# Layer B's first products of a hybrid trunk: right operands split one and a half products ahead, S2 staggered, row stores moved by two products, the fourth operand's split moved one product

## The chip, the cores and the metric

The kernel runs on one core of a Trainium2 chip. The metric is the device time of one execution in microseconds (us), the median of three runs. The profile and the trace belong to one profiled execution, and its times are counted from the start of that execution's span.

## The reference, cut to what matters

Two layers are applied to a sequence of 1024 tokens of width 1024, each as `h = h + W_out(mixer(RMSNorm(h)) * silu(z))`; a final RMSNorm follows.

```python
hn = rmsnorm(h, norm_w[0])
z, u, v = split(hn @ a_w_in, 3)                  # 1024 x 6144, layer A
mixed = einsum(w_causal, layernorm(v)) + b_s     # chunks of 128 tokens
h = h + (u * mixed * silu(z)) @ a_w_out          # 2048 x 1024
hn = rmsnorm(h, norm_w[1])
proj = hn @ b_w_in                               # layer B: z (2048), x (2048), B and C (1024 each), dt (32)
xbc = silu(causal_depthwise_conv(x, B, C))       # 4 taps
# chunked state-space scan over 128-token chunks, gate by silu(z), grouped RMSNorm
h = h + gated @ b_w_out
out = rmsnorm(h, final_norm_w)
```

The change lies in the middle: the end of layer A's output product, and the part of `proj` that gives z and half of x, B and C.

## The kernel before, in words

**Products.** Large matrix products are done by one level of a seven-product scheme (Winograd's form of Strassen's): left and right operand are cut into 2 x 2 blocks, sums of blocks are formed, and seven half-size products, numbered 1 to 7, are added up into the four results C11, C12, C21, C22. The matmuls take their operands in the type fp32r. To keep the accuracy of float32, each operand is split into a high part (a cast on ACT, `hh` on the left and `wh` on the right, in `split`, L111, or L109 where the sign is turned) and a low part (the rest, a subtraction on DVE, `hl` and `wl`, L112 or L110). A product is then three matmuls, high by high, low by high and high by low (`mm3`, L134, L135, L136).

**Class `Block`.** One Block is one set of columns of a weight matrix. Its right operands come from four loaded quarters (`load`, queued by SP, L120). `prep(n)` makes product n's `wh` and `wl`; both come from pools with three buffers. `sums_a` and `sums_b` begin the operand sums t1 and t2: ACT writes a negated quarter (L211, L212, L217), then DMAs queued by POOL add other quarters to it in memory (L202). Product 6 uses t2, product 5 t1. `mm(n, i)` does one half (`unit`) of product n, 12 matmuls of 128 x 512; products 6 and 7 go on adding to the accumulators of product 1, so these must have been copied away first. `post(n, i)` does what follows a half: for products 1, 6 and 7 an ACT copy of the accumulator to `u` (L292), for the others a result: a DVE sum (L972 for z columns, L1320 for x, B and C) and what is to be done to it later.

**Results.** For z columns ACT applies Silu (L977) and stores on its own DMA queue (L978). For x, B and C the result goes through the four-tap convolution: one ACT pass (L1287), three DVE taps (L1281 with a few edge columns in L1284), then Silu (L1312) and a store (L1313), both on ACT.

**The stages around the change.** The order of each engine's instructions is the order in which the Python code issues them; in these stages it is written out by hand, and each engine is given its own list of it.

- Layer A's output product (class `Out`, 560 to 692 us) goes through products 1, 7, 2, 6, 4, 5, 3 in steps `c` of 0 to 3. At each step `hook_a` does side work; `store_h1(0, c, 0)` stores a row block of the new h on ACT's DMA queue (L913). At the end of product 6 ACT copies its four accumulators to `u` (L855), and product 4 adds to the same accumulators.
- `into_b` (692 to 775 us) normalises and transposes the rows of h, makes the left operands of layer B (A11, A12, A22, S1 to S4), and runs the seven products of the first z block in between. S2, the left operand of product 6, is made for four token tiles: a DVE difference (L1085), ACT's high part (L109) and DVE's low part (L110); the S3 differences are L1080.
- `blocks` (777 to 1040 us) runs six more blocks (z1, x01, z2, bc01, x35, bc35, each in the order 1, 2, 6, 7, 5, 4, 3) and the narrow block z3 (1, 2, 6, 5, 7, 3, 4). Between the halves come one step of the `decays` list (dt, softplus and cumulative sums, DVE L1215 to L1238) and the results that are waiting.
- After that come `scans` with the remaining projections (accumulators `ab`), to about 1440 us, and layer B's output product. The first of these projections needs the fourth left operand A21, which `rest_a21` reads back from DRAM (`f01`, `f` in the profile, SP L1337) and splits (ACT L111 and DVE L112 on 128 x 2048).

Of the kernel before, what the change touches and what calls it, by code (L numbers as in the profile page):

```python
# [29 lines left out]
def kernel(  # L30
# [34 lines left out]
    def s8(shape, name, dt=F32):  # L65
        return sb.tile(shape, dt, name=name, tag="s8", bufs=16)
# [39 lines left out]
    def split(hi, lo, src, eng=None, sign=1.0):  # L106

        if sign < 0:
            nc.scalar.mul(hi, src, sign)  # L109
            return nc.vector.scalar_tensor_tensor(lo, src, sign, hi.bitcast(F32), ALU.mult, ALU.subtract)  # L110
        nc.scalar.copy(out=hi, in_=src)  # L111
        return (eng or nc.vector).tensor_tensor(out=lo, in0=src, in1=hi.bitcast(F32), op=ALU.subtract)  # L112
# [491 lines left out]
    for g in range(G):  # L604
# [26 lines left out]
        def mix(m, th):  # L631
            c = g * 2 + m
            mx = sm("mx")
            for q in range(4):
# [11 lines left out]
        blk = Block(HS, lambda kh, j: [a_w_in[kh * 512:(kh + 1) * 512, j * DI + g * 256:j * DI + (g + 1) * 256]],  # L646
                    False, done_zu)
# [263 lines left out]
    def store_h1(th, tt, nb):  # L911
        queue = nc.sync if nb else nc.scalar
        queue.dma_start(out=h1_d[th * 4 + tt][:, nb * 512:(nb + 1) * 512], in_=ao.row(th, tt, nb))  # L913

    def hook_a(n, c):
        if n == 1:
            ao.fetch(1, min(c + 2, 3))
        elif n == 7:
            ao.fetch(2, c), ao.fetch(22, c)
        elif n in (2, 6, 4):  # L920
            if n > 2:
                ao.fetch({6: 4, 4: 5}[n], c)
                store_h1(0, c, 0) if n == 6 else None
            ao.sums(n, c)
            if (n, c) == (6, 3):
                ao.b12_plus(0, 0)
        else:
            ao.prep_last(c)
            store_h1(1, c, 0)

    def from_a():

        blk.prep(3)
        for c in range(2):
            ao.fetch(1, c)
        ao.prep(1, 0)
        mix(0, 1)
        blk.mm(3, 0)
        mix(1, 1)
        blk.mm(3, 1)  # L940
        for n in (1, 7, 2, 6, 4):
            for i, _ in enumerate(ao.product(n, hook_a)):
                if n == 1 and i in (0, 2):
                    mix(i // 2, 0)
                    if i == 2:
                        store()
# [12 lines left out]
    def finish():  # L959

        while late:
            late.pop(0)()
# [61 lines left out]
    def into_b():  # L1024
# [4 lines left out]
        blk = zb[0]  # L1029
        nrm, F, TP, st = {}, {}, {}, {}  # L1030
# [15 lines left out]
        def part(name, tt):  # L1046
            return [m[:, :, tt * P:(tt + 1) * P] for m in H2[name]]
# [29 lines left out]
        def s3(tt):  # L1077
            if tt == 0:
                st["s3"] = s8([P, 4, 4, P], "s3")
            TTv(out=st["s3"][:, tt], in0=F[1, tt][:, 0], in1=F[0, tt][:, 0], op=ALU.subtract)  # L1080

        def s2(tt):

            f0 = F[1, tt][:, 0]
            TTv(out=f0, in0=f0, in1=F[0, tt][:, 1], op=ALU.subtract)  # L1085
            split(*part("S2", tt), f0, sign=-1.0)
            if tt % 2:
                f = st[tt // 2]
                Gp.dma_start(out=f[:, :, 1], in_=f[:, :, 0], accum_op=ALU.add)
# [8 lines left out]
        for n, _ in enumerate(ao.product(5, hook_a)):  # L1098
            if n == 8:
                ao.prep_unit(0)  # L1100
# [50 lines left out]
        blk.fourth()  # L1151
        blk.eng = None
        blk.prep(4)
        s3(3)
        for i in range(2):
            blk.mm(2, i, False)
        for tt in range(4):
            s2(tt)
        blk.prep(6)
        blk.post(1, 0), blk.post(1, 1)  # L1160
        for tt in range(4):
            both("S3", tt, st["s3"][:, tt])
        dt_post(1, pd)
# [17 lines left out]
        nxt = zb[1]  # L1181
# [108 lines left out]
    def xbc_block(kind, gs):  # L1290

        held, halos = {}, {}

        def cols(j):
            if kind == "x":
                return [(DI + gs[j] * 256, 256)]
            return [(2 * DI + j * 1024 + g * P, P) for g in gs]

        def W(kh, j):
            return [b_w_in[kh * 512:(kh + 1) * 512, c:c + n] for c, n in cols(j)]  # L1300

        def out(th, i, j, src, halo=None):
            if kind == "x":
                g, m, c = gs[j], i, cols(j)[0][0] + i * P
            else:
                g, m, c = gs[i], 2 + j, cols(j)[i][0]
            dst = k2([P, 512], "xc")
            for op in conv_ops(dst, src, (c - DI) // P, halo):
                op()

            def rest():
                nc.scalar.activation(dst, dst, AF.Silu)  # L1312
                nc.scalar.dma_start(out=xbc_d[g][:, th, m, :], in_=dst)  # L1313

            return rest

        def done(name, i, a, u):
            th, j = 2 - int(name[1]), int(name[2]) - 1
            if u is not None:
                nc.vector.tensor_tensor(out=u, in0=a, in1=u, op=ALU.add)  # L1320
                a = u
            if th == 0:
                halo = halos[i, j] = tiny([P, 8], "halo")[:, 0:3]
                nc.vector.tensor_copy(out=halo, in_=a[:, 509:512])
                todo.append(lambda: out(0, i, j, a))
                if (i, j) in held:
                    todo.append(lambda: out(1, i, j, held[i, j], halo))
            elif (i, j) in halos:
                todo.append(lambda: out(1, i, j, a, halos[i, j]))
            else:  # L1330
                held[i, j] = a

        return Block(H2, W, False, done, None)

    def rest_a21():
        raw = s8([P, 4, 512], "f01")
        nc.sync.dma_start(out=raw, in_=f01_d)  # L1337
        yield
        H2.update(new_H(("A21",)))
        split(*H2["A21"], raw)  # L1340
# [79 lines left out]
    def blocks():  # L1420


        ORDER, LAST = (1, 2, 6, 7, 5, 4, 3), (1, 2, 6, 5, 7, 3, 4)
        for g in SPILT:
            xbc_d[g] = dr.tile([P, 2, 4, 512], F32, name=f"xbc_d{g}")
        pairs = SPILT[:2], SPILT[2:]
        bs = [zb[1], xbc_block("x", pairs[0]), zb[2], xbc_block("bc", pairs[0]), xbc_block("x", pairs[1]),
              xbc_block("bc", pairs[1]), zb[3]]
        seq = [(k, n) for k in range(len(bs)) for n in (ORDER if k < len(bs) - 1 else LAST)]
        small, turn, a21 = decays(), [0], rest_a21()  # L1430

        def unit(b, n, i):

            turn[0] += 1
            off = late[:]
            late.clear()
            if b is bs[-1]:
                if n in (1, 6, 7):
                    late.append(todo.pop(0)())
            elif next(small, 0) == 0 and todo and (turn[0] % 2 or len(todo) > 3):  # L1440
                late.append(todo.pop(0)())
            b.mm(n, i, b is not bs[-1] or n != 5)
            if b is bs[-1] and n == 7:
                b.post(5, i)
            for f in off:
                f()

        for at, (k, n) in enumerate(seq[1:], 1):
            b, nxt = bs[k], bs[k + 1] if k + 1 < len(bs) else None
            if at + 1 < len(seq):  # L1450
                k2_, n2 = seq[at + 1]
                if n2 not in bs[k2_].Y:
                    bs[k2_].prep(n2)
            if n == 2:
                b.fourth()
            if nxt is not None:
                if n == 1 or at == 1:
                    nxt.load(0, 1)
                if n == 6:
                    nxt.load(0, 0)  # L1460
                elif n == 7:
                    nxt.sums_a()
                elif n == 5:
                    nxt.load(1, 0)
                    nxt.sums_b()
                elif n == 4:
                    nxt.load(1, 1)
            elif n == 6:
                next(pj)
            elif n == 5:  # L1470
                next(a21)
            elif n == 4:
                next(pj)
            for i in range(b.units):
                unit(b, n, i)
        finish()
        next(a21, None)

    with tc.manual_schedule():
        into_b()  # L1480
        blocks()
# [482 lines left out]
```

## Time and profile before

| | |
|---|---|
| three runs | 1590.07, 1592.04, 1591.79 us; median 1591.79 |
| profiled execution | 1599.45 us, of which the span is 1597.6 us |
| TensorE (PE) busy | 1503.3 us, 94% of the span |
| DVE, ACT, POOL busy | 1063.6, 782.9 and 420.2 us |
| mean granted TensorE clock | 0.975 |
| output product of layer A | 560 to 692 us |
| `into_b` | 692 to 775 us |
| `blocks` | 777 to 1040 us |

The span is what the trace covers; the profiled execution's own time is 1.85 us longer, and 7.66 us (0.5%) above the median of the runs. PE stands for TensorE's matmuls, ACTq or SPq for the DMA issues of that engine, and `u<-acc` for an instruction that reads the tile `acc` and writes `u`. A bracket such as `[2.64 <-ACT u L292]` says that the engine sat idle for 2.64 us ahead of the instruction, and that the idle time was ended by ACT's instruction on line 292.

### The profile page before, as it was taken

What the parts mean: (1) busy time and instruction counts of PE and PEld (TensorE: products, weight loads), DVE (VectorE), ACT (ScalarE), POOL (GpSimd) and SP (SyncE); (2) the same over time, 40 slices, a digit from 0 to 9 for tenths busy, and PEclk for the clock granted to TensorE, in tenths of its full rate; (3) what the DMA queues carried; (4) which work ended last, traced back from release to release, by engine and by line L of the source; (5) the groups of instructions that cost most, each with busy time, mean ns of one, the idle gap of its engine ahead of it and who ended that gap; (6) DMA issues with size and microseconds to landing.
All of it is one profiled execution on the core that took longest, in us unless ns stands there. A gap on an engine that the chain in (4) does not pass through costs nothing.

```text
span 1597.6 us, 21214 instructions
## 1 busy us (share of the span) xinstructions
PE 1503.3 (94%) x7830; PEld 1239.6 (78%) x7830; DVE 1063.6 (67%) x1701; ACT 782.9 (49%) x1251; POOL 420.2 (26%) x441
## 2 busy tenths in 40 slices
PE   5799999999999999998999999989999999987997
PEld 4799988888888887776788787767777777766876
DVE  7976566666666644777737377646776666777876
ACT  4522232332323354655555555546666666755363
POOL 3601110000000131210011312116766666532121
PEclk8899999999999999999999999999999999998999
DMA  5154323322333999856367878666566464677872
GB/s 174 41 174 143 106 98 111 111 98 98 110 110 111 329 262 245 191 128 139 99 159 178 165 165 158 162 188 188 162 180 179 133 183 126 198 270 167 221 139 105
DMA packets 174839, 251.82 MB, mean 158 GB/s; under 512 B 16288, under 2 KB 102928, under 8 KB 171536
## 3 DMA queue, kind: packets, MB, share of 16 engines
q1 hardware_dynamic: 124120, 168.39, 33.9%
q0 software_dynamic: 39520, 63.19, 20.5%
q10 hardware_dynamic: 11096, 18.90, 3.3%
q8 instruction: 62, 1.02, 0.3%
q14 instruction: 41, 0.34, 0.1%
HBM read 185.61 MB, written 51.18 MB: 148 GB/s over the span
## 4 chain that ended last, share of the span: by engine, by line
PE 59%; issue 15%; DVE 10%; ACT 7%; DMA 6%; POOL 1%; SPq 1%; ACTq 1%; POOLq 0%; DVEq 0%
PE acc L136 10%; PE acc L134 9%; PE acc L135 9%; PE ab L134 4%; PE ab L136 4%; PE ab L135 4%; PE yy L1571 2%; PE yy L1575 2%; DVE wl L112 2%; PE bo L135 2%; PE bo L134 2%; PE bo L136 2%; PE ao L134 2%; PE ao L135 2%; PE ao L136 2%
## 5 line engine op out<-in xcount | busy, mean ns | idle before, releaser
L134 PE MATMUL acc<-hh,wh 128*128 128x512 f32 x868 | 343.2, 395 | 15.0 <-ACT u L292 7.2
L136 PE MATMUL acc<-hh,wl 128*128 128x512 f32 x868 | 341.7, 394 | 2.2 <-DVE wl L112 2.1
L135 PE MATMUL acc<-hl,wh 128*128 128x512 f32 x868 | 340.2, 392 | 0.0
L134 PEld LDWEIGHTS acc<-hh,wh 128*128 128x128 f32 x868 | 164.6, 190 | 51.9 <-ACT u L292 8.9
L112 DVE TENSOR_TENSOR wl<-wr,wh 128x1024 fp32r<-128x1024 f32 (+1 forms) x97 | 115.6, 1193 | 125.8 <-ACT wh L111 125.8
L136 PEld LDWEIGHTS acc<-hh,wl 128*128 128x128 f32 x868 | 164.5, 189 | 39.9 <-DVE wl L112 5.5
L135 PEld LDWEIGHTS acc<-hl,wh 128*128 128x128 f32 x868 | 164.5, 190 | 33.4
L111 ACT CAST wh<-wr 128x1024 fp32r<-128x1024 f32 (+1 forms) x113 | 116.5, 1031 | 103.1 <-PE acc L135 56.7
L292 ACT COPY u<-acc 128x512 f32<-128x512 f32 x117 | 67.7, 583 | 200.1 <-PE acc L136 198.5
L136 PE MATMUL acc<-wh,hl 128*128 128x256 f32 x448 | 131.7, 294 | 12.4 <-DVE hl L395 12.4
L134 PE MATMUL ab<-hh,wh 128*128 128x512 f32 x288 | 129.5, 450 | 7.2 <-DVE x L1281 3.8
L134 PE MATMUL acc<-wh,hh 128*128 128x256 f32 x448 | 132.5, 296 | 3.8 <-DVE vt L331 2.1
L135 PE MATMUL acc<-wl,hh 128*128 128x256 f32 x448 | 130.9, 292 | 1.3 <-DVE wl L405 1.3
L135 PE MATMUL ab<-hl,wh 128*128 128x512 f32 x288 | 114.3, 397 | 3.2 <-DVE hl L112 3.2
L136 PE MATMUL ab<-hh,wl 128*128 128x512 f32 x288 | 115.2, 400 | 0.0
L136 PEld LDWEIGHTS acc<-wh,hl 128*128 128x128 f32 x448 | 90.2, 201 | 13.5 <-DVE hl L395 13.5
L134 PEld LDWEIGHTS acc<-wh,hh 128*128 128x128 f32 x448 | 90.4, 202 | 4.8 <-ACT wh L111 2.3
L135 PEld LDWEIGHTS acc<-wl,hh 128*128 128x128 f32 x448 | 90.5, 202 | 1.7 <-DVE wl L405 1.5
L134 PE MATMUL bo<-wh,xh 128*128 128x512 f32 x192 | 78.5, 409 | 8.0 <-ACT wh L111 7.2
L112 DVE TENSOR_TENSOR xl<-ya,xh 128x1024 fp32r<-128x1024 f32 x40 | 49.9, 1246 | 53.1 <-ACT xh L111 53.1
L1544 ACT ACTIVATE wl<-wl,tk 128x128 f32<-128x128 f32 x256 | 81.5, 391 | 0.6 <-DMA wl<-cs_d 0.3
L645 POOL DMA_DIRECT2D y_d<-y x8 | 4.4, 548 | 290.9 <-DVE y L642 290.9
(320 smaller groups left out, 3284.0 us busy)
## 6 DMA issues: line engine op xcount, KB each, us to landing
wr<-in_a_w_in_dram SPq DMA_DIRECT2D x48, 512.0 KB, 3.8
wl<-cs_d SPq DMA_DIRECT2D x64, 256.0 KB, 3.4
wr<-in_b_w_in_dram SPq DMA_DIRECT2D x30, 512.0 KB, 5.1
wb<-in_a_w_out_dram SPq DMA_DIRECT2D x10, 1024.0 KB, 11.2
wb<-in_b_w_out_dram SPq DMA_DIRECT2D x10, 1024.0 KB, 8.0
wr<-in_b_w_in_dram SPq DMA_DIRECT2D x36, 256.0 KB, 5.7
v<-v_d SPq DMA_DIRECT2D x8, 1024.0 KB, 5.0
y_d<-y POOLq DMA_DIRECT2D x8, 1024.0 KB, 5.6
```

The lines of the kernel that those rows point to most:

```text
L111: nc.scalar.copy(out=hi, in_=src)
L112: return (eng or nc.vector).tensor_tensor(out=lo, in0=src, in1=hi.bitcast(F32), op=ALU.subtract)
L134: nc.tensor.matmul(out=o, lhsT=l[0], rhs=r[0], start=start, stop=False, **kw)
L135: nc.tensor.matmul(out=o, lhsT=l[0], rhs=r[1], start=False, stop=False, **kw)
L136: nc.tensor.matmul(out=o, lhsT=l[1], rhs=r[0], start=False, stop=stop, **kw)
L292: nc.scalar.copy(out=self.u[n][:, i], in_=a)
L645: store = lambda: nc.gpsimd.dma_start(out=y_d[-1], in_=y)
L1544: nc.scalar.activation(wl[:, j, :], wl[:, j, :], AF.Relu, scale=-1.0, bias=tokc(2, c, self.g)[:, j:j + 1])
L1571: nc.tensor.matmul(out=yy[f * 64:(f + 1) * 64, pt * P:(pt + 1) * P], lhsT=w[:, j * 64:(j + 1) * 64], rhs=wl[:, j, :], start=True, stop=True)
L1575: nc.tensor.matmul(out=yy[:, 256 + pt * P:384 + pt * P], lhsT=self.state[c - 1][:, pt * P:(pt + 1) * P], rhs=self.x(3, c), start=True, sto ...
```

## The change

Four edits are made; no arithmetic is added or taken away, and PE, POOL and SP keep their instructions in the same order. What changes is the place of instructions of ACT and DVE.

1. The four row stores L913 of layer A's output product move from product 6 to product 4.
2. In `into_b`, S2's difference (`s2_a`) and its split (`s2_b`) become two functions. The differences run ahead of the splits, and the copies of product 1's accumulators (L292) are issued ahead of S2 rather than behind it.
3. In `blocks`, `ahead(at + 2)` after a product's first half makes the right operand for the product after the next; before, an operand was made at the start of the product ahead of its own. `sums_a` moves from the start of product 7 to behind its first half.
4. The split of A21 moves from behind `finish()`, after the last block, to the start of that block's product 4, its last one.

```diff
@@ hook_a
-                store_h1(0, c, 0) if n == 6 else None
+                store_h1(0, c, 0) if n == 4 else None
@@ into_b
-        def s2(tt):
+        def s2_a(tt):
             f0 = F[1, tt][:, 0]
             TTv(out=f0, in0=f0, in1=F[0, tt][:, 1], op=ALU.subtract)
-            split(*part("S2", tt), f0, sign=-1.0)
+
+        def s2_b(tt):
+            split(*part("S2", tt), F[1, tt][:, 0], sign=-1.0)
...
         blk.prep(4)
-        s3(3)
+        blk.post(1, 0), blk.post(1, 1)
+        s2_a(0), s3(3), s2_a(1)
         for i in range(2):
             blk.mm(2, i, False)
-        for tt in range(4):
-            s2(tt)
+        s2_b(0), s2_a(2), s2_b(1), s2_a(3), s2_b(2), s2_b(3)
         blk.prep(6)
-        blk.post(1, 0), blk.post(1, 1)
@@ blocks
+        def ahead(at):
+            if at < len(seq):
+                k, n = seq[at]
+                if n not in bs[k].Y:
+                    bs[k].prep(n)
...
-            if at + 1 < len(seq):
-                k2_, n2 = seq[at + 1]
-                if n2 not in bs[k2_].Y:
-                    bs[k2_].prep(n2)
+            ahead(at + 1)
...
-                elif n == 7:
-                    nxt.sums_a()
...
             elif n == 4:
                 next(pj)
+                next(a21, None)
             for i in range(b.units):
                 unit(b, n, i)
+                if i == 0:
+                    if nxt is not None and n == 7:
+                        nxt.sums_a()
+                    ahead(at + 2)
         finish()
-        next(a21, None)
```

**Block z1, products 6 and 7, DVE.** `dtw` and `dtr` are the tiles of the `decays` list, `wr` and `t` raw right operands and sums, `zt` a z result. Before:

```order
529 L972 TENSOR_TENSOR zt<-acc,u 128x512
530 L1215 TENSOR_SCALAR dtw<-dtw 128x256
531 L1216 RECIPROCAL dtw<-dtw 128x256
532 L1217 TENSOR_TENSOR dtw<-dtw 128x256
533 L1218 TENSOR_TENSOR dtw<-dtw 128x256
534 L1219 TENSOR_SCALAR dtw<-dtw 128x256
535 L1223 SCALAR_TENSOR_TENSOR dtw<-dtw 128x256 x3
536 L972 TENSOR_TENSOR zt<-acc,u 128x512
537 L260 TENSOR_TENSOR wr<-wr 128x1024
538 L112 TENSOR_TENSOR wl<-wr,wh 128x1024
539 L1223 SCALAR_TENSOR_TENSOR dtw<-dtw 128x256 x4
```

With the change (line numbers after the edit are up to 6 higher):

```order
528 L972 TENSOR_TENSOR zt<-acc,u 128x512
529 L260 TENSOR_TENSOR wr<-wr 128x1024
530 L112 TENSOR_TENSOR wl<-wr,wh 128x1024
531 L1216 TENSOR_SCALAR dtw<-dtw 128x256
532 L1217 RECIPROCAL dtw<-dtw 128x256
533 L1218 TENSOR_TENSOR dtw<-dtw 128x256
534 L1219 TENSOR_TENSOR dtw<-dtw 128x256
535 L1220 TENSOR_SCALAR dtw<-dtw 128x256
536 L1224 SCALAR_TENSOR_TENSOR dtw<-dtw 128x256 x3
537 L972 TENSOR_TENSOR zt<-acc,u 128x512
538 L1224 SCALAR_TENSOR_TENSOR dtw<-dtw 128x256 x4
```

Product 7's operand (L260, L112) now stands ahead of the `decays` step and of the second `zt` sum. On ACT the same place reads, before:

```order
344 L977 ACTIVATE zt<-zt 128x512
345 L978 DMA z_d_5288<-zt 128x512
346 L111 CAST wh<-wr 128x1024
347 L292 COPY u<-acc 128x512
348 L977 ACTIVATE zt<-zt 128x512
349 L978 DMA z_d_5288<-zt 128x512
350 L292 COPY u<-acc 128x512
351 L111 CAST wh<-t_6194 128x1024
```

With the change:

```order
343 L111 CAST wh<-wr 128x1024
344 L977 ACT_TABLE_LOAD
345 L977 ACTIVATE zt<-zt 128x512
346 L978 DMA z_d_5288<-zt 128x512
347 L292 COPY u<-acc 128x512
348 L977 ACTIVATE zt<-zt 128x512
349 L978 DMA z_d_5288<-zt 128x512
350 L111 CAST wh<-t_6194 128x1024
351 L292 COPY u<-acc 128x512
```

Product 7's cast went up to the front, and product 5's cast (from `t`) now stands ahead of the copy of product 6's second half (the last L292 shown).

**Block z2, products 7, 5 and 4, ACT.** Before:

```order
430 L211 ACTIVATE t_6906<-wr 128x1024
431 L212 ACTIVATE wr<-wr 128x1024
432 L1287 ACTIVATE xc<-u,par 128x512
433 L292 COPY u<-acc 128x512 x2
434 L1312 ACTIVATE xc<-xc 128x512
435 L1313 DMA xbc_d_6209<-xc 128x512
436 L111 CAST wh<-wr 128x1024
437 L217 ACTIVATE t_6906<-wr 128x1024
```

With the change:

```order
431 L1288 ACTIVATE xc<-u,par 128x512
432 L292 COPY u<-acc 128x512
433 L211 ACTIVATE t_6928<-wr 128x1024
434 L212 ACTIVATE wr<-wr 128x1024
435 L111 CAST wh<-wr 128x1024
436 L292 COPY u<-acc 128x512
437 L1313 ACTIVATE xc<-xc 128x512
438 L1314 DMA xbc_d_6209<-xc 128x512
439 L217 ACTIVATE t_6928<-wr 128x1024
```

The cast `wh<-wr` of product 4 stood behind the Silu `xc<-xc` and its store; it now stands ahead of them and of the copy of product 7's second half.

**The end of `blocks`, ACT.** Before:

```order
577 L111 CAST wh<-wr 128x1024 x2
578 L977 ACTIVATE zt<-zt 128x512
579 L978 DMA z_d_5292<-zt 128x512
580 L111 CAST wh<-wr 128x1024
581 L977 ACTIVATE zt<-acc 128x512
582 L1287 ACTIVATE xc<-u,par 128x512
583 L978 DMA z_d_5292<-zt 128x512
584 L111 CAST hh<-f_8048 128x2048
```

With the change:

```order
584 L111 CAST wh<-wr 128x1024
585 L111 CAST hh<-f_8048 128x2048
586 L977 ACTIVATE zt<-zt 128x512
587 L111 CAST wh<-wr 128x1024
588 L978 DMA z_d_5292<-zt 128x512
589 L977 ACTIVATE zt<-acc 128x512
590 L111 CAST wh<-wr 128x1024
591 L978 DMA z_d_5292<-zt 128x512
592 L1288 ACTIVATE xc<-u,par 128x512
```

A21's cast (`hh<-f`) moved ahead of both last z results; its DVE half (L112, 128 x 2048) moved ahead of the convolution taps in the same way.

## The prediction

> **What bounds the kernel now.** I read the page first, then the waits of PE in the stretch that the diff touches, then the granted clock behind each wait.
>
> ```profile
> PE 1503.3 (94%) x7830; PEld 1239.6 (78%) x7830; DVE 1063.6 (67%) x1701; ACT 782.9 (49%) x1251; POOL 420.2 (26%) x441
> PE 59%; issue 15%; DVE 10%; ACT 7%; DMA 6%; POOL 1%; SPq 1%; ACTq 1%; POOLq 0%; DVEq 0%
> ```
>
> PE does the work and no matmul is removed, so a gain can only come out of PE's pauses. These are PE's waits between 630 and 1060 us (total, times, longest):
>
> ```profile
> PE acc L134 <- ACT u L292: 7.0, 3, 3.9
> PE acc L134 <- ACT wh L111: 5.6, 4, 2.1
> PE ao L134 <- ACT u L855: 3.9, 1, 3.9
> PE ab L135 <- DVE hl L112: 3.2, 1, 3.2
> PE acc L136 <- DVE wl L112: 2.1, 4, 0.5
> PE acc L134 <- DVE zt L972: 2.1, 1, 2.1
> PE ab L134 <- ACT zt L977: 1.5, 1, 1.5
> ```
>
> They sum to 25.4 us. Every one but the last two rows is a wait for work that the diff moves. Behind the pauses stands a second loss, seen in stretches of the trace (engines' busy time; the third number from the end is the granted clock):
>
> ```profile
> 560.00:630.00 70.00, 70.00 (x311) 57.95 (x310) 36.22 (x38) 36.92 (x43) 19.64 (x22) 1.00 1.07 251
> 641.40:645.00 3.60, 3.55 (x9) 2.79 (x10) 3.06 (x5) 3.34 (x5) 3.44 (x5) 0.53 1.05 381
> 743.20:746.80 3.60, 3.55 (x9) 2.54 (x10) 3.33 (x6) 3.09 (x6) 0.00 (x0) 0.60 0.82 141
> 791.30:795.00 3.70, 3.70 (x9) 2.65 (x10) 3.49 (x9) 3.27 (x5) 0.03 (x1) 0.56 0.62 179
> 884.30:888.00 3.70, 3.17 (x13) 2.30 (x14) 2.38 (x3) 2.37 (x3) 2.36 (x4) 1.00 1.34 234
> 965.70:969.20 3.50, 3.50 (x11) 2.68 (x10) 3.40 (x6) 0.44 (x1) 3.50 (x4) 0.51 1.25 238
> 1006.60:1010.10 3.50, 3.37 (x8) 2.69 (x9) 3.43 (x7) 1.10 (x2) 2.22 (x2) 0.52 0.71 124
> 1048.50:1055.40 6.90, 6.83 (x18) 5.40 (x19) 2.39 (x7) 0.63 (x1) 0.00 (x0) 0.56 0.74 217
> ```
>
> While PE is fed, the clock is 1.00 for 70 us on end, 70.00/311 = 0.225 us a matmul, 2.7 us a half of 12. After most pauses it is near half for about 3.5 us. I price such a stretch as its length by what is missing from the clock: 3.6 x 0.47 = 1.7 us after the first. A pause costs its wait plus 0.16, since the wait counts from the end of a matmul of 0.39 us, while the next start was due 0.23 after the last.
>
> **The change, part by part.** Gains are counted positive.
>
> (1) The row stores. ACT's instructions at the end of layer A's product 6:
>
> ```profile
> 632.86 1.05 ACT L111 CAST wh<-wb 128x1024 fp32r<-128x1024 f32 x1
> 638.64 0.33 ACTq L913 DMA_DIRECT2D h_d<-u  x1
> 639.01 1.91 ACT L711 ACTIVATE wb<-wb 128x2048 f32<-128x2048 f32 x1 [5.10 <-DMA u<-in_x_dram]
> ```
>
> The idle 5.10 us end with the landing of an SP load, which neither L711 nor the stored rows use. [...] L711, the four copies L855 and PE's product 4 queue behind it. [...] The gain is 3.9 + 0.16 + 1.7 = 5.8. If another wait holds ACT there, the gain is nil.
>
> (2) S2 in the first z block:
>
> ```profile
> 735.13 0.63 ACT L109 ACTIVATE hh<-f 128x512 fp32r<-128x512 f32 x1 [2.50 <-DVE f L1085]
> 737.12 0.63 ACT L109 ACTIVATE hh<-f 128x512 fp32r<-128x512 f32 x1 [1.36 <-DVE f L1085]
> 741.64 1.03 ACT L111 CAST wh<-t 128x1024 fp32r<-128x1024 f32 x1
> 742.57 1.07 ACT L292 COPY u<-acc 128x512 f32<-128x512 f32 x2
> ```
>
> A tile takes 1.99 us, handed from DVE to ACT and back; the copies that PE waits for come last. They now come first, which ends that wait: 4.1, and 3.6 x 0.40 = 1.4 of clock. But product 6 then waits for S2 itself. Staggered, DVE goes through nine operations of 128 x 512 back to back, 0.60 us apart (as L260 follows L972 in z1's rows below), from about 734 to 739.4; the casts for product 6 end about 739.7 and `wl` about 741.0, where PE could start at 739.1 (743.2 less the pause). After that ACT and DVE feed PE with no slack: repeating the rows' durations in the new order, product 5, which in the trace waits 0.39 for `wh` and 0.53 for `wl` (the smallest of the `wh` and `wl` waits above), starts about 3.4 us sooner. I take 3.4; the bounds are 1.5 (half of the handing back and forth stays) and 5.5 + 1.2 = 6.7 (all pauses gone).
>
> (3) Operands in the six blocks. First z1, where a new wait arises:
>
> ```profile
> 787.87 0.68 DVE L972 TENSOR_TENSOR zt<-acc,u 128x512 f32<-128x512 f32 x1
> 788.47 1.21 DVE L260 TENSOR_TENSOR wr<-wr 128x1024 f32<-128x1024 f32 x1
> 789.72 1.04 ACT L111 CAST wh<-wr 128x1024 fp32r<-128x1024 f32 x1 [4.59 <-DVE wr L260]
> 790.67 0.58 ACT L292 COPY u<-acc 128x512 f32<-128x512 f32 x1
> 791.30 0.50 PE L134 MATMUL acc<-hh,wh 128*128 128x512 f32 x1 [2.64 <-ACT u L292]
> ```
>
> L260, the cast and `wl` go ahead of the `decays` step. This frees the first copy: 2.8 + 3.7 x 0.44 = 4.4. The price: DVE's second `zt` comes 1.21 + 1.04 + 1.23 = 3.5 later, at about 791.4; its Silu, product 5's cast and the copy of product 6's second half follow on ACT, in that order, to 794.6. PE's second half of product 7 is due at 791.2, so it waits 3.4 and, by the rows above, loses another 1.7: net -0.7, between +1.5 (Silu not held up as long) and -2.5.
>
> In z2, x35 and bc35 the wait is for product 4's operand:
>
> ```profile
> 882.16 0.63 ACT L1312 ACTIVATE xc<-xc 128x512 f32<-128x512 f32 x1 [1.64 <-DVE xc L1284]
> 883.18 1.04 ACT L111 CAST wh<-wr 128x1024 fp32r<-128x1024 f32 x1 [0.40 <-ACT xc L1312]
> 884.28 0.50 PE L134 MATMUL acc<-hh,wh 128*128 128x512 f32 x1 [2.15 <-ACT wh L111]
> 885.54 0.50 PE L136 MATMUL acc<-hh,wl 128*128 128x512 f32 x1 [0.53 <-DVE wl L112]
> ```
>
> The cast waits behind a Silu, which waits for the convolution. In the new order it stands ahead of both, behind the copy of product 7's first half and two sums: 884.28 less 2.5 of pause and three halves of 2.7 puts the end of that half at 873.7, and 0.6 + 1.05 + 1.05 + 1.04 later, about 877.5, the cast is done. Gains: z2 2.3 + 0.7 = 3.0, and 0.6 for a copy in its product 7 (the three `u` waits sum to 7.0: 3.9, 2.64 and a last of 0.4); x35, wait 1.92, 2.1 + 0.7 + 3.5 x 0.49 = 4.5; bc35, wait 1.17, 1.3 + 0.7 + 3.5 x 0.48 = 3.7. In the other blocks casts are early already; at most nothing is gained, and ACT's order can cost: I take 1.5 off (0 to 4), for x01, whose ACT store now queues behind an SP load's semaphore, and for bc01, next.
>
> ```profile
> 901.76 0.59 ACT L292 COPY u<-acc 128x512 f32<-128x512 f32 x1 [1.60 <-PE acc L136]
> 902.97 1.05 ACT L111 CAST wh<-t 128x1024 fp32r<-128x1024 f32 x1 [0.62 <-DMA t<-in_b_w_in_dram]
> ```
>
> Here the cast already waits for POOL's adding DMA. Asked half a product (2.7 us) sooner it waits about 3, with the copy at 901.76 behind it; PE needs that copy only after product 2, 5.4 us on, so it is covered by product 2.
>
> (4) A21:
>
> ```profile
> 1030.66 0.52 SPq L1337 DMA_DIRECT2D f<-f_d  x1
> 1042.67 1.90 ACT L111 CAST hh<-f 128x2048 fp32r<-128x2048 f32 x1
> 1046.24 2.27 DVE L112 TENSOR_TENSOR hl<-f,hh 128x2048 fp32r<-128x2048 f32 x1
> 1048.57 0.79 PE L135 MATMUL ab<-hl,wh 128*128 128x512 f32 x1 [3.19 <-DVE hl L112]
> xbc<-xbc_d SPq DMA_DIRECT2D x8, 1024.0 KB, 8.3
> ```
>
> The load is issued at 1030.66; by a load of the same size it lands 8.3 later, about 1039. The cast then runs to 1041 and `hl` to 1043.3, ahead of the 1045.2 (1048.57 less 3.35) at which PE wants it: gain 3.35 + 6.9 x 0.44 = 6.4. The last z result `zt<-acc`, the 1.5-us wait in the list, gets the 1.90 of the cast ahead of it and may slip by 0.4: 6.0. If the load lands at its bound, 1042 (the cast in the trace no longer waits), the slip is about 4 and the gain 2.
>
> Sum: 5.8 + 3.4 - 0.7 + 3.6 + 4.5 + 3.7 - 1.5 + 6.0 = 24.8. The profiled execution would take 1599.45 - 24.8 = 1574.7. It stands 0.5% above the runs' median of 1591.79, which becomes **1567**.
>
> The clock terms are the least certain. [...] The rows differ: pauses of 2.1 and 1.3 us before 965 and 1006 were followed by 0.51 and 0.52, one of 2.3 us before 884 by 1.00. [...]
>
> **The rivals.** *The wait moves on.* ACT takes its list in order, so each earlier cast delays something; were ACT and DVE the bound through these blocks, only (1), (4) and the z2, x35 and bc35 waits without their clock would go: 5.8 + 2 + 3 + 2.8 + 2 = 15.6, less 4 for the copies, about 12: 1580. For it speak z1 and S2, where they do set the pace; against it, that ACT is 49% busy.
>
> *Slower.* An operand cast for product 6 waits on ACT for POOL's adding DMAs, and holds the copy of product 1's second half beyond product 2. It decides once `t` lands over 5.4 us after the request: product 6 starts late, and the half clock follows. At 9 us that is 3.6 + 1.7 of clock + 1.05 for the cast = 6.3 a block, 32 in five blocks, against 24.8 gained: 1599. From 8.3 us on the loss shows (28 in five blocks). Against it: only bc01 shows any wait for `t`, of 0.62.
>
> *Nothing comes of it.* The shorter stretch is given back where loads in the scans, not PE, set the end; then 1591. Against it: the chain has DMA at 6%, and SP's loads there are issued as buffers come free, so they move up with the rest.
>
> **How the numbers follow.** A difference under 0.2%, 3.2 us, counts as none here. The forecast's case (15 to 33 us gained) has 0.72, the moved wait (4 to 15) 0.17, nothing 0.05, slower 0.06. Its own best end is 24.8 + 3.3 (all of S2) + 5.1 (no new wait in z1) = 33: 1559. Its low end, all costs at their bad bound, is 24.8 - 1.9 - 1.8 - 2.5 - 4.0 = 14.6: 1577; the range goes on to 1583 for part of the moved wait. Faster 0.89, same 0.05, slower 0.06.
>
> **What would show it.** Step by step: no wait of PE for L855; a wait for `wl` or S2 of 1 to 2 us near 739 in place of 3.94; a wait of about 3 us before the second half of z1's product 7; no wait for `wh` in z2, x35 and bc35; no wait for `hl` near 1040; stretches at half clock fewer by five or six. It is wrong if ACT shows waits for `<-DMA t` of over 3 us with copies behind them, or if PE's busy share does not rise.

## The result, and the profile after

The changed kernel takes 1575.26 us (median of four runs, 1569.9 to 1578.1) against 1591.91 before: ratio 0.9887, 95% interval 0.9853 to 0.9922. A second set of runs of the same kernel gave 0.9904 (0.9889 to 0.9920). The change gains 15 to 18 us, where 24.8 were forecast: the measured time lies inside the range that the prediction gave, 1559 to 1583, but the forecast of 1567 is lower than any run. The profiled execution took 1573.5 us, within 1.2 us of the 1574.7 that the sum gave for it; why both hold is the question of the next sections.

The page of the changed kernel, engines' busy time and the chain of work that ended last:

```profile
PE 1488.6 (95%) x7830; PEld 1229.6 (78%) x7830; DVE 1065.0 (68%) x1701; ACT 782.2 (50%) x1251; POOL 421.6 (27%) x441
PE 63%; issue 15%; DVE 10%; ACT 6%; DMA 4%; POOL 1%; ACTq 0%; SPq 0%; POOLq 0%; DVEq 0%
```

PE's waits between 630 and 1060 us in the changed kernel (total, times, longest):

```profile
PE tp L1260 <- ACT tk L1263: 6.0, 1, 6.0
PE acc L134 <- ACT u L292: 3.6, 2, 3.1
PE acc L134 <- DVE zt L972: 2.1, 1, 2.1
PE acc L136 <- DVE wl L112: 1.4, 3, 0.5
PE acc L134 <- ACT wh L111: 1.1, 2, 0.6
PE ab L134 <- ACT zt L977: 0.7, 1, 0.7
```

Set against the list of before, the waits for L855 (3.9) and for `hl` (3.2) are gone, those for `wh` fell from 5.6 to 1.1, and the sum of the rows fell from 25.4 to 14.9. One row is new and now the largest: PE stands 6.0 us before L1260. That line is a transpose of the `decays` list on PE; L1263 is ACT's copy of a finished transpose out of PSUM (`tk`, L1262 before). The transposes take turns in two PSUM buffers, so the third needs the copy of the first.

Where ACT is late, in block x01 of the changed kernel:

```profile
797.07 0.59 ACT L977 ACTIVATE zt<-acc 128x512 f32<-128x512 f32 x1
801.86 0.33 ACTq L978 DMA_DIRECT2D z_d<-zt  x1
802.23 0.49 ACT L1255 COPY dtw<-dtw 128x128 f32<-128x128 f32 x2 [4.57 <-DMA ecs_d<-dtw]
802.63 0.59 ACT L977 ACTIVATE zt<-acc 128x512 f32<-128x512 f32 x1
807.26 0.33 ACTq L978 DMA_DIRECT2D z_d<-zt  x1
807.63 1.04 ACT L111 CAST wh<-wr 128x1024 fp32r<-128x1024 f32 x1 [4.40 <-DMA cs_d<-cs]
808.58 0.37 ACT L1263 COPY tk<-tp 128x256 f32<-128x256 f32 x1
```

The Silu of a z1 result ends at 797.7, but its store is issued at 801.86, and the next store stands as long. Each ends with the landing of somebody else's DMA, as at the row store in layer A's output product (5.10 us of idle time there): ACT's idle 4.57 us end with an `ecs_d` store of SP, its 4.40 us, by the bracket at the cast L111 behind the second store, with a `cs_d` store of SP. L1263 queues behind both, and PE behind L1263 (6.0 us). The granted clock after the two long pauses of the changed kernel, in z1 (783.2) and in x01 (809.0):

```profile
783.20:786.80 3.60, 3.60 (x16) 2.98 (x17) 3.15 (x9) 1.93 (x3) 0.00 (x0) 1.00 0.00 0
809.00:812.50 3.50, 3.50 (x10) 2.88 (x11) 1.53 (x2) 0.84 (x2) 0.00 (x0) 0.52 0.56 207
```

So x01 lost 6.1 of pause and 3.5 x 0.48 = 1.7 of clock, 7.8 in all. The trace of the kernel before held the same wait in small, under cover:

```profile
813.68 0.33 ACTq L978 DMA_DIRECT2D z_d<-zt  x1
814.05 0.37 ACT L1262 COPY tk<-tp 128x256 f32<-128x256 f32 x1 [3.78 <-DMA z_d<-zt]
815.42 0.38 PE L1259 MATMUL tp<-ident,cs 128*128 128x128 f32 x2
```

ACT stood 3.78 us before a store there too, in that case for an earlier store of its own. PE did not notice, because the third transpose (the last line) was not due yet; but the copy ended at 814.4, so the cover left was only 1.0 us.

The other steps, in the changed kernel: the copies at the end of product 6, product 4's cast in z2, and A21's cast with the last z result.

```profile
631.49 1.91 ACT L711 ACTIVATE wb<-wb 128x2048 f32<-128x2048 f32 x1
633.30 1.54 ACT L855 COPY u<-ao 128x512 f32<-128x512 f32 x3
871.10 1.03 ACT L111 CAST wh<-wr 128x1024 fp32r<-128x1024 f32 x1
1020.54 1.91 ACT L111 CAST hh<-f 128x2048 fp32r<-128x2048 f32 x1
1023.81 0.59 ACT L977 ACTIVATE zt<-acc 128x512 f32<-128x512 f32 x1
```

L711 follows the casts without a gap; z2 shows no wait for `wh` any more; A21's cast is done before the last z result, which PE now awaits 0.7 instead of 1.5.

### The profile page after: what moved, and what is told of

It is laid out like the page before. It is cut to its first block, busy times and chain, and to the rows that moved or that the text cites. A ratio compares the mean times of both kernels' runs of the same rounds, so it can differ in the third digit from the quotient of the medians.

```text
span 1571.6 us, 21215 instructions
## 1 busy us (share of the span) xinstructions
PE 1488.6 (95%) x7830; PEld 1229.6 (78%) x7830; DVE 1065.0 (68%) x1701; ACT 782.2 (50%) x1251; POOL 421.6 (27%) x441
## 4 chain that ended last, share of the span: by engine, by line
PE 63%; issue 15%; DVE 10%; ACT 6%; DMA 4%; POOL 1%; ACTq 0%; SPq 0%; POOLq 0%; DVEq 0%
PE acc L136 10%; PE acc L134 9%; PE acc L135 9%; PE ab L134 4%; PE ab L136 4%; PE ab L135 4%; PE ao L135 3%; PE ao L134 3%; PE ao L136 3%; PE yy L1577 2%; PE yy L1581 2%; DVE wl L112 2%; PE bo L135 2%; PE bo L134 2%; PE bo L136 2%
## 5 line engine op out<-in xcount | busy, mean ns | idle before, releaser
L112 DVE TENSOR_TENSOR wl<-wr,wh 128x1024 fp32r<-128x1024 f32 (+1 forms) x97 | 115.6, 1193 | 129.6 <-ACT wh L111 129.4
L292 ACT COPY u<-acc 128x512 f32<-128x512 f32 x117 | 68.0, 583 | 207.1 <-PE acc L136 205.7
L111 ACT CAST wh<-wr 128x1024 fp32r<-128x1024 f32 (+1 forms) x113 | 116.4, 1030 | 98.4 <-PE acc L135 58.8
L112 DVE TENSOR_TENSOR xl<-ya,xh 128x1024 fp32r<-128x1024 f32 x40 | 49.8, 1246 | 51.2 <-ACT xh L111 51.2
```

Source lines behind the costliest of these rows:

```text
L292: nc.scalar.copy(out=self.u[n][:, i], in_=a)
```

## The experiments

All ratios are to the kernel before, timed on the same chip in the same set.

| kernel | us, median | ratio (95%) |
|---|---|---|
| changed kernel, second set | 1576.76 | 0.9904 (0.9889 to 0.9920) |
| row stores back | 1583.24 | 0.9939 (0.9915 to 0.9963) |
| S2 back | 1582.33 | 0.9926 (0.9897 to 0.9954) |
| operands and `sums_a` back | 1583.15 | 0.9925 (0.9896 to 0.9955) |
| A21 back | 1581.32 | 0.9925 (0.9908 to 0.9942) |
| `decays` stores on POOL | 1570.30 | 0.9864 (0.9848 to 0.9880) |
| z1's halves first | 1575.59 | 0.9897 (0.9876 to 0.9918) |
| the last two and z3 | 1571.31 | 0.9865 (0.9847 to 0.9883) |
| before, `decays` stores on POOL | 1592.12 | 0.9996 (0.9977 to 1.0014) |

The four kernels with one edit undone are 3.3 to 5.6 us slower than the changed kernel by these ratios, and the interval of each still touches that of the changed kernel. What one edit is worth is therefore read from its stage in the profiles.

### Each edit undone

The row stores back in product 6:

```diff
-                store_h1(0, c, 0) if n == 4 else None
+                store_h1(0, c, 0) if n == 6 else None
```

> The changed kernel with the four row stores back in product 6 of layer A's output product; the other edits stay. Theory (each pause is its own): the wait of PE for L855 of about 3.9 us and some 3.5 us at half clock return there, 5.8 us in that stage, and the stages behind it keep their pauses: about 1581 against 1575. Rival (the waits move on, since ACT takes its list in order): undoing it costs under 3 us, because the stores also hold ACT back in product 4.

PE's waits show, beside those of the changed kernel (x01's is now 4.3):

```profile
PE tp L1260 <- ACT tk L1263: 4.3, 1, 4.3
PE ao L134 <- ACT u L855: 3.9, 1, 3.9
```

The pause is back as in the first profile. From the first matmul of the output product to the first transpose of `into_b` (L1042) it takes 143.85 us, against 138.3 in both profiles of the changed kernel: 5.5, for 5.8 forecast. The rival falls.

S2 as before:

```diff
-        blk.post(1, 0), blk.post(1, 1)
-        s2_a(0), s3(3), s2_a(1)
+        s3(3)
         for i in range(2):
             blk.mm(2, i, False)
-        s2_b(0), s2_a(2), s2_b(1), s2_a(3), s2_b(2), s2_b(3)
+        for tt in range(4):
+            s2_a(tt), s2_b(tt)
         blk.prep(6)
+        blk.post(1, 0), blk.post(1, 1)
```

> The changed kernel with S2's differences and splits one after the other and the copies of product 1 behind them, as before; the other edits stay. Theory: the wait for L292 of 3.9 us and half a clock return in the first z block, while the four waits of 0.5 to 0.6 us around products 6 and 5 go from four to two; net 3.4 us in that stage, about 1579. Rival: ACT and DVE set the pace of this stage whichever way S2 is written, and the stage is within 1 us of the changed kernel's.

```profile
PE acc L134 <- ACT u L292: 7.1, 2, 4.0
PE tp L1261 <- ACT tk L1264: 3.9, 1, 3.9
```

The wait of 4.0 is back; the second row is the pause in x01, one line lower in this kernel. From L1042 to the first matmul of product 5 it takes 65.0 us; the changed kernel takes 60.7, the first profile of before 64.1. The edit is worth 3.4 to 4.3, so the rival falls. That ACT and DVE do set the pace once S2 is staggered shows in the waits of 0.5 to 0.6 that are left for `wh`, `wl` and `u`.

Right operands and `sums_a` as before:

```diff
+                elif n == 7:
+                    nxt.sums_a()
...
-                if i == 0:
-                    if nxt is not None and n == 7:
-                        nxt.sums_a()
-                    ahead(at + 2)
```

> The changed kernel with the right operands made at the start of the product ahead, and sums_a at the start of product 7, as before; the other edits stay. Theory: the pause of 6.0 us in x01 (PE's L1260 behind ACT's L1263, behind two ACT stores) and its half clock go away, 7.8 us; z1's pause goes back to the first half of product 7 (2.6 us, half clock); the waits for wh of 1.2 to 2.2 us before product 4 of z2, x35 and bc35 come back with their clock, 11.8 us. Net 3 to 5 us slower than the changed kernel, about 1579. Rival (the x01 pause comes from something else that the changed kernel has, such as the stage being reached sooner while the DMAs are not): the pause in x01 stays over 4 us and the time is about 1586.

```profile
PE acc L134 <- ACT wh L111: 6.6, 5, 2.2
PE acc L134 <- ACT u L292: 3.5, 3, 2.6
```

The pause in x01 is gone (ACT still stands 3.4 us before a store there, under cover), and the waits for `wh` in z2, x35 and bc35 are back. From L1042 to the first projection it takes 347.6 us, against 340.0 and 342.4 in the two profiles of the changed kernel. The edit gains 5 to 8 there and brings the pause in x01 along; the rival falls. The runs give 3.3 us, within the 3 to 5 expected; the profiled execution, 1585.35 us, is one of the two longest of five.

A21's split back behind the last block:

```diff
-                next(a21, None)
...
         finish()
+        next(a21, None)
```

> The changed kernel with A21's split back behind the last block; the other edits stay. Theory: PE waits 3.2 us for hl before the first projection, with about 7 us near half clock behind it, and the wait for the last z result stays under 2: 6 us slower, about 1581. Rival (the wait for the last z result grows by what the cast ahead of it takes, so the move wins half at most): 3 us or less.

```profile
PE ab L135 <- DVE hl L112: 3.2, 1, 3.2
PE ab L134 <- ACT zt L977: 1.4, 1, 1.4
```

Both waits are as before. The runs say 0.9925 against 0.9904 for the changed kernel, 3.3 us, and the intervals just overlap: the 6 of the theory are not reached, and the times do not part it from the rival's 3. The rival's mechanism does not show: with the cast ahead of it the last z result is awaited 0.7, without it 1.4. The clock behind `hl` was 0.77 over 6.9 us in this profile, a loss of 1.6 where the theory has 7 us near half clock; the last profiles, with 1.00 there twice, show that the loss can be nothing.

### The pause in x01

The changed kernel itself, for a second profile:

> The changed kernel again, word for word, for a second profile and five more rounds. If the pauses are set by the order of the instructions (theory), PE's waits are the same to 0.1 us everywhere but in x01, where a DMA's landing ends the wait, and the time is 1574 to 1578; the profiled executions' gain of 26 us was then partly luck of the two executions profiled. If pauses come and go between executions (rival), other waits show.

All waits came back to 0.2 us, but for x01 (4.1 instead of 6.0) and one more of 0.6 near 980. The clock behind the pause in z1 was 1.00 in the first profile and 0.71 here:

```profile
783.30:786.80 3.50, 3.50 (x11) 2.83 (x12) 3.15 (x9) 1.83 (x3) 0.00 (x0) 0.71 0.00 0
```

So in these two profiles the pauses came back with the order of the instructions, while the wait that a DMA's landing ends (6.0 and 4.1) and the clock behind z1's pause (1.00 and 0.71) did not.

Then the eight small stores of the `decays` list (`cs_d` and `ecs_d`) were queued by POOL instead of SP:

```diff
-                nc.sync.dma_start(out=cs_d[2 * q:2 * q + 2].rearrange("c h l -> h c l"),
+                nc.gpsimd.dma_start(out=cs_d[2 * q:2 * q + 2].rearrange("c h l -> h c l"),
...
-                nc.sync.dma_start(out=ecs_d[:, q * 256:(q + 1) * 256], in_=ecs[rs_, :])
+                nc.gpsimd.dma_start(out=ecs_d[:, q * 256:(q + 1) * 256], in_=ecs[rs_, :])
```

> [...] Theory: ACT's two stores in x01 no longer wait 4.4 and 4.6 us, PE's wait of 6.0 us before L1260 falls under 1, with its half clock: 6 to 8 us faster than the changed kernel. Rival (those DMAs land late because the DMA engines are full, and the copies L1263 wait for something that depends on them): the wait stays over 4.

Its ACT at the same place, and PE's wait:

```profile
796.49 0.59 ACT L977 ACTIVATE zt<-acc 128x512 f32<-128x512 f32 x1
797.11 0.33 ACTq L978 DMA_DIRECT2D z_d<-zt  x1
800.90 0.60 ACT L977 ACTIVATE zt<-acc 128x512 f32<-128x512 f32 x1 [2.93 <-DMA z_d<-zt]
801.53 0.33 ACTq L978 DMA_DIRECT2D z_d<-zt  x1
PE tp L1260 <- ACT tk L1263: 0.8, 1, 0.8
```

Each store now leaves as its Silu ends (the second Silu still waits 2.93 for an earlier store to land), PE's wait fell to 0.8, and the kernel is 6.5 us faster than the changed one of the same set, with intervals that do not touch. The same bytes are moved, so their mere amount is not the cause. What ties ACT's stores to these eight, and whether SP's load, which no longer stands behind them in SP's queue, had a part in it, this run does not show. To see that these stores cost nothing by themselves, the same edit was made in the kernel before:

> The kernel before with only the eight small stores of the decays list queued by POOL instead of SP. In the kernel before, PE has no pause in x01. Theory (the stores cost time only because the earlier casts brought ACT's stores onto their semaphores): within 2 us of the kernel before, ratio 0.999 to 1.001. Rival (the stores on SP cost time in any case, and the gain of 6.5 us has nothing to do with the change): 4 us or more faster, ratio under 0.9975.

The ratio is 0.9996, and the rival's 0.9975 lies just outside its interval. In this run's profile ACT's covered wait ahead of L1262 fell from 3.78 to 0.46 us: the stores make ACT wait in the kernel before as well. They cost time only once the earlier casts let PE's transposes arrive ahead of ACT.

### The remaining pauses

z1's halves issued ahead of the `decays` step:

```diff
+            first = b is bs[0]
+            if first:
+                b.mm(n, i)
             if b is bs[-1]:
...
-            b.mm(n, i, b is not bs[-1] or n != 5)
+            if not first:
+                b.mm(n, i, b is not bs[-1] or n != 5)
```

> The changed kernel with z1's halves issued ahead of the step of the decays list instead of behind it, so that DVE's second zt sum is not behind reciprocal and polynomial. Theory: PE's wait of 3.1 us before the second half of z1's product 7 goes, nothing else changes: 3 us faster. Rival (ACT is late there by itself, with product 5's cast ahead of the copy): over 2 us of wait remain.

```profile
PE tp L1260 <- ACT tk L1263: 6.3, 1, 6.3
PE acc L136 <- DVE wl L112: 2.4, 5, 0.5
PE ab L134 <- ACT zt L977: 1.5, 1, 1.5
```

The wait of 3.1 in z1 went, as the theory has it, but the waits for `wl` grew by 1.0, that in x01 was 6.3 and that for the last z result 1.5, as if PE came sooner to work that was not ready sooner. The time is the changed kernel's within the intervals; the expected 3 us are not shown.

All three edits together (z3: the convolution's step issued behind product 5's sums in product 7):

```diff
-                if n in (1, 6, 7):
+                if n in (1, 6):
...
                 b.post(5, i)
+                late.append(todo.pop(0)())
```

> Both of the last two edits, and in z3 the convolution's step issued behind product 5's sums in product 7 instead of ahead of them, so that PE's product 3 does not wait 2.1 us for DVE's zt. Theory (pauses add up): 6 to 8, 3 and 2 us, together 11 to 13 us faster than the changed kernel, about 1563. Rival (ACT and DVE have no room left, so waits turn up elsewhere): under 6.

```profile
PE ab L134 <- ACT zt L977: 2.6, 1, 2.6
PE tp L1260 <- ACT tk L1263: 1.4, 1, 1.4
PE acc L134 <- DVE zt L972: 1.4, 1, 1.4
```

It is 5.5 us faster than the changed kernel, where 11 to 13 were expected, and no faster than the stores on POOL alone. In z3 the wait for `zt` fell by 0.7, and that for the last z result is 2.6, against 1.3 and 1.5 with each of the other two edits alone. This fits the rival, that ACT and DVE have no room left there; no run makes the edit in z3 alone. The version with the stores on POOL has the lowest median of these, 1570.3 us.

### Two more profiles of the kernel before

> The kernel before, word for word, for a second profile. The first profiled execution took 1599.45 us, 7 us more than the median of the timed runs, and the profile of the changed kernel 1573.5. Theory: PE's waits between 630 and 1060 us are the same list as in the first profile (25 us in all, to 1 us), and what differs between executions lies elsewhere (the first 550 us, the half-clock stretches): then the forecast's sum was right for its execution and wrong for the runs by what lies there. Rival: the waits themselves differ, by 5 us or more, and the first profile was not typical of this stage.

> The kernel before once more, a third profile, to see the spread of the stages; the same two theories as for the second.

They took 1590.31 and 1591.31 us. PE's waits are those of the first profile, to 0.3 us in each row of the list, but for one: L855's was 1.7 in the second (with 0.8 lost for `wl` earlier, near 580) and 4.0 in the third. The granted clock behind the same pauses is not the same. Second profile, behind L855, in the first z block, z1, z2, x35, bc35 and behind `hl`:

```profile
637.60:641.10 3.50, 3.28 (x14) 2.74 (x15) 2.78 (x4) 3.50 (x6) 3.35 (x5) 1.00 1.03 388
737.90:741.40 3.50, 3.43 (x9) 2.68 (x10) 3.24 (x6) 3.16 (x7) 0.00 (x0) 0.56 0.87 150
786.00:792.20 6.20, 6.19 (x15) 4.75 (x16) 5.96 (x14) 5.74 (x8) 2.52 (x2) 0.50 0.53 138
880.20:883.70 3.50, 2.98 (x7) 2.08 (x8) 2.37 (x3) 2.17 (x3) 2.17 (x3) 0.60 1.35 232
962.90:966.40 3.50, 3.50 (x11) 2.69 (x9) 3.40 (x6) 0.45 (x1) 3.50 (x4) 0.52 1.21 223
1002.70:1006.20 3.50, 2.97 (x12) 2.16 (x13) 3.43 (x6) 2.17 (x3) 2.57 (x2) 1.00 0.41 108
1046.00:1052.90 6.90, 6.83 (x30) 5.66 (x31) 2.38 (x7) 0.63 (x1) 0.00 (x0) 1.00 0.82 211
```

Third profile, the same places:

```profile
639.90:643.40 3.50, 3.47 (x9) 2.78 (x10) 2.98 (x4) 3.33 (x5) 3.35 (x5) 0.59 1.00 356
741.40:744.90 3.50, 3.46 (x8) 2.45 (x9) 3.24 (x6) 3.12 (x6) 0.00 (x0) 0.55 0.86 147
789.40:792.90 3.50, 3.41 (x8) 2.65 (x9) 3.33 (x8) 3.07 (x6) 0.00 (x0) 0.52 0.57 154
882.40:885.90 3.50, 2.97 (x12) 2.15 (x13) 2.39 (x3) 2.17 (x3) 2.15 (x3) 1.00 1.34 233
963.60:967.10 3.50, 3.50 (x10) 2.67 (x9) 3.39 (x6) 0.62 (x1) 3.50 (x4) 0.51 1.20 229
1003.60:1007.10 3.50, 2.98 (x12) 2.16 (x13) 3.43 (x6) 2.17 (x3) 2.57 (x2) 1.00 0.41 107
1046.90:1053.80 6.90, 6.84 (x30) 5.69 (x31) 2.38 (x7) 0.63 (x1) 0.00 (x0) 1.00 0.86 225
```

Behind `hl`, where the first profile lost 3.0 us to the clock after a pause of 3.2, the two others lost nothing after the same pause; in bc35 likewise, 1.7 against nothing. In z1 the second profile stayed at half clock for 6.2 us, the two others for about 3.5. Behind PE's wait of 2.1 us for `zt` in z3, which no edit touches, the first profile shows 1.00 over 3.5 us, and the two others 0.53 and 0.51, a loss of 1.6 to 1.7 each. The stages of the five profiles, worked out from the starts of PE's first matmul in each (us):

| | output product to L1042 | L1042 to first projection | projection to layer B's output product | the rest |
|---|---|---|---|---|
| before, first profile | 144.1 | 349.5 | 358.5 | 745.5 |
| before, second | 141.8 | 352.2 | 354.1 | 740.4 |
| before, third | 144.0 | 349.6 | 354.1 | 741.8 |
| changed, first | 138.3 | 340.0 | 352.0 | 741.3 |
| changed, second | 138.3 | 342.4 | 348.9 | 744.2 |

The first three columns hold all that the diff touches. On the means of the profiles the change gains 5.0, 9.3 and 5.2 in them, 19.5 in all; the rest differs by up to 5 us between executions of one kernel. Between L1042 and the first projection, where the waits of before agree, the clock priced as above took 6.4, 9.3 and 6.7 us in its three profiles, and that is how the column's 349.5, 352.2 and 349.6 differ.

## Why the prediction was right and wrong

**Right: the list of pauses, and what happens to each.** The row stores gave 5.5 for 5.8. S2 gave 3.4 to 4.3 for 3.4, with the small waits that the hand schedule left. In z1 the pause moved to the second half of product 7: 3.1 where 3.4 was forecast. The waits for `wh` in z2, x35 and bc35 went. A21's split came in time, and the last z result did not slip. PE's busy share rose, from 94% to 95%. In bc01 the other sign that the prediction gave for being wrong did come: ACT's cast waited well over 3 us for POOL's adding DMA, with a copy behind it.

```profile
896.64 1.05 ACT L111 CAST wh<-t 128x1024 fp32r<-128x1024 f32 x1 [5.39 <-DMA t<-in_b_w_in_dram]
```

PE lost 0.30 us to it, waiting for `wl` (0.47 in the second profile): product 2 covered the rest, as the prediction's own bound of 5.4 us has it. So the sign of 3 us was set too low, and in this block the cover was used up. The rivals that the waits move on and that the change makes the kernel slower did not come about as the main effect, but the first did take x01.

**Wrong: the term of 1.5 for x01 and bc01, bounded at 4.** The place was named, and ACT's two stores there did stand until a DMA of SP landed (4.57 and 4.40 us); the size was 5.8 to 7.8, made of 4.1 to 6.0 of pause and 1.7 of clock. The prediction gives no working for its 1.5. The step that failed is that it named the store at which ACT stops and not what stands behind that store in ACT's list, the copy L1263 that PE's third transpose needs; in the trace of before ACT's 3.78 us lay under cover, with 1.0 us to spare.

**Wrong: the clock terms.** Stretches at half clock were counted in full from one execution: 1.7 + 1.4 + 1.6 + 1.7 + 1.7 + 3.0 = 11.1 of the gains. Priced in the same way, the second profile of before has 1.5 + 3.1 + 1.4 + 1.7 = 7.7 at these places, the third 1.4 + 1.6 + 1.7 + 1.7 = 6.4. At these places the first profile was the unlucky one, by 3.4 to 4.7, and the sum was made for it; scaling the sum to the runs by the ratio of the two times, 0.5%, left that in. That the profiled execution of the changed kernel came within 1.2 us of the sum is luck: from first profile to first profile the columns that the diff touches gain 5.8 + 9.5 + 6.5 = 21.8, and the other 4.2 lie in the rest. The sentence that set the rows against each other was right: pauses of 2.1 and 1.3 us were followed by 0.51 and 0.52, one of 2.3 us by 1.00. The profiles of before go further: the same pause of 3.2 us was followed by 0.56, 1.00 and 1.00.

Together: 24.8, less 4.3 to 6.3 for x01 and 3.4 to 4.7 for the clock, plus the 0.7 to 1.7 that z1's new pause lost less to the clock than the 1.7 priced (0.71 in one profile, 1.00 in the other), is 14.5 to 18.8; the runs measured 15 to 18.

## What to carry to other kernels

List not only the waits of the engine that sets the end, but the idle times of the engine that feeds it, and ask of each what stands behind it in that engine's list and how long the cover lasts once the other waits are gone. ACT, which also queues DMAs here, was stopped by transfers that have nothing to do with its own data, for 5.10 us at the row store and for 4.57 and 4.40 us in x01; moving the row stores away from the critical copies was worth 5.5 us, and moving eight small stores from SP's queue to POOL's 6.5. Count pauses from one profile, but price the slow clock behind them from several.

## What the runs showed of the hardware

The same pause was not always followed by the same clock. After 1.17 us of wait and 0.53 more in bc35 the clock was 0.52 once and 1.00 twice; after 3.2 us before `hl` it was 0.56 once and 1.00 twice; after 2.6 us in z1 it was 0.50 to 0.56 in all three profiles of before, and after 3.1 us there 1.00 and 0.71 in the two of the changed kernel. A stretch at half clock lasted about 3.5 us at most of these places, and 6.2 to 6.9 us twice: behind z1's pause in the second profile of before, and behind `hl` in the first.
